# A decoder block on one core: the first group of down products by seven products, the residual's stores, the factors at the entry of the feed-forward part

## The chip, the core and the metric

The kernel runs on one core of a Trainium2 chip. The core has a matrix engine (TensorE, "PE" in the profile, with weight loads listed as "PEld"), a vector engine (VectorE, DVE), a scalar engine (ScalarE, ACT), a general one (GpSimd, POOL) and a queue engine (SyncE, SP); 16 DMA engines move data between HBM and the on-chip memory (SBUF). Matmul results go to eight PSUM banks. Each engine runs its own list of instructions in order and waits on semaphores for what the others deliver; the order in which the program is written sets only the order of each list.

The metric is the device time of one execution, in microseconds. Before the change the median of three runs is 2143.21 us (2142.64 to 2144.26).

## The reference, cut to what matters

The kernel computes one decoder block for 512 tokens of width 2048: a norm, one projection, two attention mixers, an output projection with residual, then a SwiGLU feed-forward part with residual and a last norm. All is float32. The part that matters here:

```python
hn2 = rmsnorm(h, norm2_g)                                        # 512 x 2048
h = h + (silu(hn2 @ w_gate) * (hn2 @ w_up)) @ w_down             # hidden width 5632
return rmsnorm(h, final_g)
```

## The kernel before, in words

A float32 product is made from three matmuls on rounded halves: each operand is split into a high part (ScalarE copies it rounded) and a low part (VectorE subtracts the high one), and high x high, high x low and low x high are added up in PSUM (`mm`, L1238 to L1241). Weights stream in as units of 512 KB (`load_to`, issued on SP, five buffers `raw`) and are split half a unit at a time by `Job` (128 x 512, lines L143 and L146); a split half is what the text calls a half. In the feed-forward part TensorE spends 12 matmuls of 256 columns on a half. `next_half` hands out split halves three ahead; `later(n, f)` places f behind the n-th next half in the program, `soon` and `tick` do so in steps of quarter products.

**Gate and up.** The hidden width is cut into 44 blocks of 128 (index f). For each, gate and up are made together as a 2 x 2 block product by seven products instead of eight (Strassen's scheme in Winograd's form): the left side is (gate, up) for the two halves of the input width, the right side the two halves of width by the two halves of the 512 tokens (256 each). `quad_jobs` lists the seven weight factors P1 to P7, which are sums of the four weight units A11, A21, A22 and A12. The sums are made in place by VectorE (`comb`, L819, and L843) or, in some blocks, by an adding load from HBM on POOL's queue (`fetch`, L823). The order of the seven is ORDER0 for f = 0, ORDER1 for f = 1 and for some later blocks, ORDER for the rest. With ORDER1 the factor A11 is restored by `fetch`, with ORDER all sums are VectorE's. `product` makes one of the seven (24 matmuls), `after` puts the results together on VectorE and ScalarE, `finish` applies silu and multiplies.

**Down.** The hidden blocks are grouped by four (PH = 4, eleven groups). The down product of groups 1 to 9 is made by seven products as well: `downs` places its 56 quarter products (8 output pairs k by seven names) into the schedule behind the last block of the group, `quarter` lists their weight factors, `down7` makes six matmuls each, copies partial sums between PSUM banks on ScalarE and sends the staged results to HBM tiles `kept_sums` by adding stores on POOL. `hidden_terms` builds the right-hand terms from the hidden values that `finish` left in `held`. At its first call `down7` makes two seeding matmuls (L1145). Group 0 is made plainly: in block 4 sixteen output blocks of 24 matmuls each (`down`), four behind each of the products from the fourth on, with weights from `wdn` in two buffers `rawd`, and its results are written to the same HBM tiles by plain stores. For it, `finish` splits the hidden values of blocks 0 to 3 straight into four 512-wide slots of `ah` and `al`. Group 10 is made plainly at the end (`last`).

**The residual.** It lies in SBUF (`hs`, 16 tiles of 128 x 512) until block 1. `put_away` stores a tile to HBM on POOL's queue: eight are placed behind P1 of block 1, one per half, eight behind P1 of block 2 (`AWAY`). The last one closes that memory and opens a pool of working tiles in its place (staging tiles `stga`, hidden values `hf`, terms `x3`), and clears one fifth of each `kept_sums` tile by a store of zeros. The residual is added into the sums in blocks 5, 6, 9, 10, 13, 14, 17 and 18 (`add_residual`), and all is brought back near the end.

**The entry.** In block 0, behind P6, two per-token factors are spread over partitions by matmuls (`Spread`): inv and r2, both copied from PSUM to SBUF by ScalarE (L282), with the loading of ScalarE's silu table in between (L1420). `after(0, "P6")` reads bank P1 times r2 on VectorE (L1302); block 1's first product writes that bank next.

Some first halves are split into buffers with another offset (`even`): block 2, each odd block, and the first quarter of a down group.

Of the kernel before, what the change touches and what calls it, by code (L numbers as in the profile page):

```python
# [16 lines left out]
S = 512  # L17
# [25 lines left out]
def plan():  # L43
# [31 lines left out]
def block_kernel(ctx: ExitStack, tc: tile.TileContext, xt, wst, wdn, smalls, wg, w2c, bias, ident_in, out):  # L75
# [711 lines left out]
    dn_loads = deque((0, nb) for nb in range(KB))  # L787
    dn = {}

    def load_dn():  # L790
        if dn_loads:
            k = dn_loads.popleft()
            dn[k] = wp.tile([128, 512], F32, tag="rawd", name="rawd", bufs=2)
            sp.dma_start(dn[k], wdn[k[0], k[1]])

# [15 lines left out]
    def quad_jobs(f, names):  # L811
# [17 lines left out]
        for k in range(2):  # L829
# [10 lines left out]
            elif order(f) == ORDER1:  # L840
# [29 lines left out]

    def dn_job(p, nb):
        return Job(lambda: dn[p, nb], post=load_dn)
# [38 lines left out]
    for f in range(FB):  # L911
        qj = quad_jobs(f, order(f))
        p = f // PH - 1
        nb = 0
        for i, name in enumerate(order(f)):
            seq = sorted(((k, n) for k in range(8) for n in DTIME), key=lambda x: 7 * x[0] + DTIME[x[1]])
            if name == "P3" and f > PH and f % PH == 0:
# [3 lines left out]
            if name == "P3" and f > PH and f % PH == 0:  # L921
# [14 lines left out]
    load_dn()  # L936
    load_dn()
# [9 lines left out]
    def close_attention():  # L947
# [16 lines left out]
        def close():  # L964
# [8 lines left out]
            for _ in range(2):  # L973
                ffn.tile([128, S], F32, tag="ft", name="ft", bufs=2)
# [42 lines left out]
    def ft(name="ft"):  # L1017
        return ffn.tile([128, S], F32, tag="ft", name=name, bufs=2)

# [89 lines left out]
    dbanks = {}  # L1109
    SEEDED = ("P6", "P7")  # L1110
    AWAY = {(1, "P1"): (0, 8, 0), (2, "P1"): (8, 8, 0)}
# [29 lines left out]
    def down7(p, k, name, wh, wl):  # L1141

        if not roles:
            seed = ps.tile([128, 512], F32, tag="misc", name="pd")
            pe.matmul(seed[:, :256], ones, sm[:, :1].to_broadcast([128, 256]), start=True, stop=True)  # L1145
            roles.append((banks["P3"], banks["P4"], seed, dbanks[1]))
# [13 lines left out]
        def add(x, q, n):  # L1160
            return lambda s=sums[x]: pool_e.dma_start(kept_sums[k][:, q:q + n, :], s, accum_op=OP.add)  # L1161
# [22 lines left out]
    def hidden_terms(f):  # L1184

        i = (f - 1) % 2
        x3 = st["x3"]
        hl = [[a[:, 12:16, :].rearrange("p t (i c) -> p t i c", c=256)[:, :, i, :] for a in (ah, al)],
              [a.rearrange("p (t i c) -> p t i c", i=2, c=256)[:, :, i, :] for a in x3]]
# [7 lines left out]
        if f % PH in (1, 2):  # L1197
            top = held[f - 1]
            t = st["pool"].tile([128, 1, 256], F32, tag="s2", name="t1", bufs=2)

            def s1():
                dve.tensor_tensor(t[:, 0, :], top[:, LO], top[:, HI], op=OP.subtract)
                hi(1, 2, 3, top[:, None, LO])

            def s2():
                lo(1, 2, 3, top[:, None, LO])
# [16 lines left out]
        def s2():  # L1223
            dve.scalar_tensor_tensor(t24[:, 0, :], t3[:, 0, :], -1.0, top[:, LO], op0=OP.mult, op1=OP.subtract)
            lo(0, 0, 2, botv)
            hi(0, 3, 4, t3)

        def s3():
            dve.scalar_tensor_tensor(t24[:, 1, :], t24[:, 0, :], -1.0, bot[:, LO], op0=OP.mult, op1=OP.subtract)
            lo(0, 3, 4, t3)  # L1230
# [12 lines left out]
    def finish(f, g, u, c):  # L1243
# [3 lines left out]
        wait = 0 if f == FB - 1 else 1 if f < 8 or f % PH else 2  # L1247
# [9 lines left out]
        def up():  # L1257
            if PH <= f <= FB - PH:
# [8 lines left out]
        if f < PH or f > FB - PH:  # L1267
# [10 lines left out]
    def after(f, name):  # L1278
# [11 lines left out]
        if name == "P1":  # L1290
            st["g"] = ft()
            if f:
                st["u"] = (st["pool"].tile([128, S], F32, tag="hf", name="hf", bufs=4)
                           if PH <= f <= FB - PH else ft())
# [28 lines left out]
    def down(ph, nb):  # L1323
        n = nb % 3
        if n not in dbanks:
            dbanks[n] = banks["P3"] if not n else (ps.tile([128, 512], F32, tag="t", name="pd", bufs=2) if n == 1 else
                                                ps.tile([128, 512], F32, tag="misc", name="pd"))
        p = dbanks[n]
        h, l = next_half()
        for c in (LO, HI):  # L1330
            for i in range(PH):
                mm(p[:, c], h[:, 128 * i:128 * i + 128], l[:, 128 * i:128 * i + 128], ah[:, 12 + i, c],
# [251 lines left out]
```

## Time and profile before

| | us |
|---|---|
| median of three runs | 2143.21 |
| the profiled execution | 2147.43 |
| its span, first to last instruction | 2145.6 |
| TensorE busy | 2128.1 |
| feed-forward blocks 0 to 8, start of block 0 to start of block 9 | 269.0 |

The profile is one execution. Times in it count from its first instruction. A row of the timeline gives start, length, engine, line, operation, output and inputs, shape, count, and in brackets the idle time of that engine ahead of it and what ended it. A row of windows gives a stretch, its length, and for each engine busy time and count of instructions (those that only reach into the stretch are counted too), then the granted TensorE clock, the DMA engines' busy share and GB/s. Matmuls overlap in the records (each is listed at 0.28 us, while they start 0.11 to 0.12 us apart), so the pace is read from counts and starts, not from durations. Buffer numbers are left out of names: the banks P1 to P7 are all "P".

### The profile page before, as it was taken

The page shows a single profiled execution, that of the slowest core. Times are in us where ns is not written, and L with a number is a line of the kernel's source. Part 1 is how long each engine was busy: PE and PEld are TensorE (multiplying, and loading weights), DVE is VectorE, ACT ScalarE, POOL GpSimd, SP SyncE. Part 2 cuts the span into 40 slices and gives each one's busy share as a digit, 9 for nine tenths or more (in the row PEclk, how much of TensorE's full clock was granted, in tenths as well). Part 3 has the DMA queues.
Part 4 walks back from the last instruction along what each step waited for, and adds up shares of the span by engine and source line. Part 5 has one row for each costly group of instructions (what it writes and reads, how often), then busy time and mean ns, then how long its engine had stood idle before and what let it go on. Part 6 is the DMA issues. An engine that isn't in the chain of part 4 may idle for free.

```text
span 2145.6 us, 41296 instructions
## 1 busy us (share of the span) xinstructions
PE 2128.1 (99%) x15346; PEld 1988.0 (93%) x15346; DVE 1629.4 (76%) x3460; ACT 1241.6 (58%) x2973; POOL 321.9 (15%) x378
## 2 busy tenths in 40 slices
PE   9999999999999999999999999999999999999997
PEld 7888888888888888999999999999999999999997
DVE  6755656366657678856989898898989898988885
ACT  6544444344445256444675858585767667675856
POOL 0000000000000001211131313131212213030323
PEclk9999999999999999999999999999999999999998
DMA  7442222322234334545596969775766758594982
GB/s 237 147 141 81 82 82 69 101 81 72 65 106 155 99 99 128 177 153 148 145 230 142 213 154 210 171 188 139 184 161 158 184 141 187 139 216 118 208 245 89
DMA packets 124347, 313.67 MB, mean 146 GB/s; under 512 B 13424, under 2 KB 35568, under 8 KB 124144
## 3 DMA queue, kind: packets, MB, share of 16 engines
q1 hardware_dynamic: 77104, 236.49, 34.9%
q0 software_dynamic: 46896, 74.47, 19.6%
q8 instruction: 120, 1.97, 0.4%
q14 instruction: 83, 0.68, 0.1%
q10 hardware_dynamic: 144, 0.07, 0.0%
HBM read 245.96 MB, written 65.01 MB: 145 GB/s over the span
## 4 chain that ended last, share of the span: by engine, by line
PE 96%; DMA 1%; DVE 1%; ACT 1%; issue 0%; SPq 0%; POOL 0%; DVEq 0%; ACTq 0%; POOLq 0%
PE P L1241 17%; PE P L1240 17%; PE P L1239 17%; PE pp L197 7%; PE pp L199 7%; PE pp L198 7%; PE pab L199 3%; PE pab L197 3%; PE pab L198 3%; PE pd L1239 2%; PE pd L1241 2%; PE pd L1240 2%; DMA raw<-in_wst_dram 1%; PE pt L568 1%; PE po L198 1%; PE pl L198 1%
## 5 line engine op out<-in xcount | busy, mean ns | idle before, releaser
L143 ACT ACTIVATE wh<-raw 128x512 fp32r<-128x512 f32 x888 | 532.7, 625 | 295.0 <-DVE raw L819 113.6
L146 DVE TENSOR_TENSOR wl<-raw,wh 128x512 fp32r<-128x512 f32 x888 | 599.3, 686 | 111.0 <-ACT wh L143 106.9
L1241 PE MATMUL P<-ah,wl 128*128 128x256 f32 x1536 | 426.1, 277 | 0.1
L1239 PE MATMUL P<-ah,wh 128*128 128x256 f32 x1536 | 425.2, 277 | 0.0
L1240 PE MATMUL P<-al,wh 128*128 128x256 f32 x1536 | 425.1, 277 | 0.0
L1241 PEld LDWEIGHTS P<-ah,wl 128*128 128x128 f32 x1536 | 288.3, 188 | 1.3 <-DVE wl L146 1.1
L1240 PEld LDWEIGHTS P<-al,wh 128*128 128x128 f32 x1536 | 288.4, 188 | 0.0
L1239 PEld LDWEIGHTS P<-ah,wh 128*128 128x128 f32 x1536 | 288.2, 188 | 0.0
L197 PE MATMUL pp<-ah,wh 128*128 128x512 f32 x640 | 260.5, 407 | 0.0
L199 PE MATMUL pp<-ah,wl 128*128 128x512 f32 x640 | 251.0, 392 | 0.0
L198 PE MATMUL pp<-al,wh 128*128 128x512 f32 x640 | 250.2, 391 | 0.0
L1161 POOL DMA_DIRECT2D sums<-stg x216 | 188.1, 927 | 312.0 <-ACT P L1155 150.0
L819 DVE TENSOR_TENSOR raw<-raw 128x512 f32<-128x512 f32 x270 | 185.7, 688 | 5.6 <-DMA raw<-in_wst_dram 2.0
L170 DVE TENSOR_TENSOR wl<-raw,wh 128x256 fp32r<-128x256 f32 x432 | 167.9, 420 | 27.3 <-ACT wh L166 25.8
L166 ACT ACTIVATE wh<-raw 128x256 fp32r<-128x256 f32 x432 | 159.2, 409 | 4.6 <-DVE raw L898 4.6
L199 PEld LDWEIGHTS pp<-ah,wl 128*128 128x128 f32 x640 | 120.2, 188 | 28.2 <-DVE wl L146 0.4
L197 PEld LDWEIGHTS pp<-ah,wh 128*128 128x128 f32 x640 | 120.5, 188 | 20.0 <-DVE tmp L369 0.5
L198 PEld LDWEIGHTS pp<-al,wh 128*128 128x128 f32 x640 | 120.6, 189 | 19.5
L555 ACT ACTIVATE e<-e,st 128x512 f32<-128x512 f32 (+1 forms) x96 | 53.7, 560 | 124.3 <-DVE st L549 124.3
L707 POOL TENSOR_TENSOR acc<-acc,osq 128x512 f32<-128x512 f32 x14 | 18.1, 1294 | 580.3 <-ACT osq L706 580.3
L1155 ACT ACTIVATE stg<-P 128x256 f32<-128x256 f32 x252 | 95.6, 381 | 12.7 <-PE P L1241 3.3
L197 PE MATMUL pab<-ah,wh 128*128 128x512 f32 x256 | 100.3, 392 | 0.0
(335 smaller groups left out, 5545.0 us busy)
## 6 DMA issues: line engine op xcount, KB each, us to landing
raw<-in_wst_dram SPq DMA_DIRECT2D x382, 512.0 KB, 4.2
sums<-stg POOLq DMA_DIRECT2D x160, 256.0 KB, 6.7
raw<-in_wst_dram POOLq DMA_DIRECT2D x42, 256.0 KB, 4.5
sums<-stg POOLq DMA_DIRECT2D x72, 128.0 KB, 6.3
bias<-in_bias_dram SPq DMA_DIRECT2D x16, 320.0 KB, 3.0
xc<-in_xt_dram SPq DMA_DIRECT2D x16, 256.0 KB, 3.5
rawd<-in_wdn_dram SPq DMA_DIRECT2D x16, 256.0 KB, 2.8
hs<-in_xt_dram SPq DMA_DIRECT2D x16, 256.0 KB, 5.7
```

Source lines behind the costliest of these rows:

```text
L143: act.activation(self.h, self.src(), AF.Copy)
L146: dve.tensor_tensor(self.l, self.src(), self.h.bitcast(F32), op=OP.subtract)
L166: act.activation(h, src(), AF.Copy)
L170: dve.tensor_tensor(l, src(), h.bitcast(F32), op=OP.subtract)
L197: pe.matmul(o, wh, mh, start=start, stop=False)
L198: pe.matmul(o, wh, ml, start=False, stop=False)
L199: pe.matmul(o, wl, mh, start=False, stop=stop)
L819: return lambda: dve.tensor_tensor(o(), o(), x(), op=OP.add)
L1161: return lambda s=sums[x]: pool_e.dma_start(kept_sums[k][:, q:q + n, :], s, accum_op=OP.add)
L1239: pe.matmul(o, wh, mh, start=start, stop=False, skip_group_check=True)
L1240: pe.matmul(o, wh, ml, start=False, stop=False, skip_group_check=True)
L1241: pe.matmul(o, wl, mh, start=False, stop=stop, skip_group_check=True)
```

## The change

- Group 0 is made like groups 1 to 9: `plan` puts its eight weight units behind block 4, the schedule calls `downs` for it, `down`, its loads and its buffers `rawd` go away, and `hidden_terms` runs from block 1 on. Its stores write instead of adding, so the clearing stores go away too. `finish` leaves blocks 0 to 3 in `held`; for their hidden values two working tiles `early` are added.
- The terms are assigned to other slots (P1 and P7 change places), so that those built in blocks 1 and 2 lie in `ah` and `al`; the difference that is built there stands in bank P3 instead of a working tile.
- The 16 stores of the residual are placed from P1 of block 1 on at 8i/5 halves, instead of eight and eight at one per half.
- Block 1 keeps ORDER1, but its factors are made as in the other form: P1 is followed by A11 + A21 on VectorE, P6 is preceded by A22 + A11 on VectorE, no `fetch`.
- In block 0 the silu table and r2 come ahead of inv, and inv's copy is placed five halves later.

```diff
-        if f > PH and f % PH == 0:
+        if f and f % PH == 0:
             p += [("dn", f // PH - 1, k) for k in range(8)]
...
-            elif order(f) == ORDER1:
+            elif order(f) == ORDER1 and f > 1:
...
-            if name == "P1" and f > PH + 1 and f % PH == 1:
+            if name == "P1" and f > PH and f % PH == 1:
                 downs(p, seq[-1:])
-            if f == PH and i > 2:
-                for _ in range(4):
-                    if nb < KB:
-                        sched.append(("d", p, nb))
-                        jobs.append(dn_job(p, nb))
-                        nb += 1
...
-    AWAY = {(1, "P1"): (0, 8, 0), (2, "P1"): (8, 8, 0)}
+    AWAY = {(1, "P1"): (0, 16, 0)}
...
-            return lambda s=sums[x]: pool_e.dma_start(kept_sums[k][:, q:q + n, :], s, accum_op=OP.add)
+            how = {"accum_op": OP.add} if p else {}
+            return lambda s=sums[x]: pool_e.dma_start(kept_sums[k][:, q:q + n, :], s, **how)
...
-            t = st["pool"].tile([128, 1, 256], F32, tag="s2", name="t1", bufs=2)
+            t = banks["P3"][:, None, :256]
...
-        wait = 0 if f == FB - 1 else 1 if f < 8 or f % PH else 2
+        wait = 0 if f == FB - 1 else 1 if f < PH or f % PH else 2
...
-            if PH <= f <= FB - PH:
+            if f <= FB - PH:
                 dve.scalar_tensor_tensor(u, u, -1.0, g, op0=OP.mult, op1=OP.mult)
                 held[f] = whole
...
-        if f < PH or f > FB - PH:
+        if f > FB - PH:
...
-            zero = pool.tile([128, 256], F32, tag="s2", name="zero", bufs=2)
-            pool_e.memset(zero, 0.0)
-            for k in range(8):
-                pool_e.dma_start(kept_sums[k][:, 2, :], zero)
...
-                later(at + i, lambda nb=first + i: put_away(nb))
+                later(at + 8 * i // 5, lambda nb=first + i: put_away(nb))
...
-        if PH < f <= FB - PH and name == order(f)[2]:
+        if 0 < f <= FB - PH and name == order(f)[2]:
...
-                st["inv"] = st["inv"]()
                 act.activation(st["rs2"].rs[:, 7, :1], ones[:, :1], AF.Silu)
                 st["r2"] = st["r2"](tag="t", bufs=2)
-                st["u"] = ft()
+                inv, pinv = st["inv"].r, st["inv"](False)
+                st["inv"] = inv
+                later(5, lambda: act.activation(inv, pinv, AF.Copy))
+                st["u"] = early()
```

More of the change, by code (lines that the diff above doesn't have):

```diff
@@ L972, in close @@
                                    for x, at in (("h", MH), ("l", ML)))
-            for _ in range(2):
-                ffn.tile([128, S], F32, tag="ft", name="ft", bufs=2)
+            for tag in ("ft", "early"):
+                for _ in range(2):
+                    ffn.tile([128, S], F32, tag=tag, name=tag, bufs=2)
             rest["hsp"] = ExitStack()
@@ L1018, in ft, with early @@
         return ffn.tile([128, S], F32, tag="ft", name=name, bufs=2)
+    def early():
+        return ffn.tile([128, S], F32, tag="early", name="early", bufs=2)
     sacc = ft("sacc")
@@ L1292, in after @@
             if f:
[L1293 to L1294 removed]
+                st["u"] = (ft() if f == 2 or f > FB - PH else early() if f == 1 else
+                           st["pool"].tile([128, S], F32, tag="hf", name="hf", bufs=4))
             else:
@@ L1321, in after @@
             finish(f, g, u, HI if f == FB - 1 else slice(0, 512))
[L1323 to L1332, printed above, removed]
-                   al[:, 12 + i, c], i == 0, i == PH - 1)
-        def add():
-            t = st["pool"].tile([128, 2, 256], F32, tag="stga", name="stg", bufs=3)
-            act.activation(t, p.rearrange("p (t c) -> p t c", c=256), AF.Copy, scale=1.0 if nb < 8 else -1.0)
-            pool_e.dma_start(mem_at(nb), t)
-        later(1, add)
     def mem_at(nb):
@@ L1379, in block_kernel @@
     for kind, a, b in sched:
-        if kind == "d":
-            down(a, b)
-            continue
         if kind == "s":
```

35 lines of the change are left out of this document (11 added, 24 removed).

## The prediction

> **What bounds the kernel now.** I read the first page, then the feed-forward part block by block (windows from one block's P1 to the next one's), then the idle time of TensorE, then the queues behind it. The page first:
>
> ```profile
> span 2145.6 us, 41296 instructions
> PE 2128.1 (99%) x15346; PEld 1988.0 (93%) x15346; DVE 1629.4 (76%) x3460; ACT 1241.6 (58%) x2973; POOL 321.9 (15%) x378
> PE 96%; DMA 1%; DVE 1%; ACT 1%; issue 0%; SPq 0%; POOL 0%; DVEq 0%; ACTq 0%; POOLq 0%
> ```
>
> TensorE is the bound: work taken from it is time, and so is each gap in it. The windows below are blocks 0, 1, 2, 3, 4 (with the first group's down products), 5, 6, 8 (second group) and 16 (fourth group). The columns are the stretch and its length, then busy time and count of each engine, granted clock, DMA share and GB/s.
>
> ```profile
> 836.00:859.61 23.61, 22.62 (x193) 22.42 (x191) 19.57 (x49) 17.90 (x39) 1.98 (x3) 1.00 0.49 134
> 859.61:878.84 19.23, 19.23 (x168) 19.23 (x169) 15.65 (x29) 8.81 (x17) 9.33 (x16) 1.00 0.60 183
> 878.84:903.68 24.84, 22.00 (x171) 21.49 (x170) 19.88 (x35) 11.90 (x24) 4.58 (x9) 0.93 0.69 241
> 903.68:923.49 19.81, 19.81 (x170) 19.81 (x169) 17.28 (x31) 10.59 (x21) 0.00 (x0) 1.00 0.37 108
> 923.49:988.50 65.01, 65.01 (x554) 65.01 (x553) 33.01 (x55) 28.68 (x53) 10.72 (x15) 1.00 0.44 146
> 988.50:1007.61 19.11, 19.11 (x170) 19.11 (x169) 13.27 (x24) 10.52 (x22) 1.95 (x2) 1.00 0.55 163
> 1007.61:1027.46 19.85, 19.84 (x171) 19.64 (x170) 17.81 (x34) 10.61 (x22) 2.39 (x2) 1.00 0.66 163
> 1046.57:1105.01 58.44, 58.44 (x502) 58.39 (x501) 51.23 (x118) 45.95 (x133) 20.18 (x24) 1.00 0.81 184
> 1280.33:1336.81 56.48, 56.48 (x500) 56.48 (x499) 50.74 (x117) 45.47 (x132) 20.03 (x24) 1.00 0.82 190
> ```
>
> A plain block holds 7 x 24 = 168 matmuls and needs 19.1 us (block 5); block 16 holds 168 + 55 x 6 = 498 in 56.48 us, 113.4 ns each. Block 2 is 5.7 us too long. Its gaps, in the order of time on TensorE (start, length, then the idle time in brackets and who ended it):
>
> ```profile
> 859.61 0.39 PE L1239 MATMUL P<-B11h,wh 128*128 128x256 f32 x1 [0.99 <-DVE ft L1302]
> ...
> 883.81 0.38 PE L1239 MATMUL P<-T4h,wh 128*128 128x256 f32 x1 [2.01 <-ACT wh L143]
> ...
> 885.14 0.39 PE L1241 MATMUL P<-T4h,wl 128*128 128x256 f32 x1 [0.83 <-DVE wl L146]
> ...
> 886.08 0.41 PE L1240 MATMUL P<-T4l,wh 128*128 128x256 f32 x1
> 886.29 0.41 PE L1241 MATMUL P<-T4h,wl 128*128 128x256 f32 x1
> ```
>
> Block 2's second product waits 2.01 and 0.83 us for its split weights, and then matmuls start 0.21 us apart (886.08 to 886.29) while the granted clock averages 0.93 over the block. The Trainium skill (TensorE: Matmul & The Clock Gate, Part 1) says that about 3.4 us of idling drops the array to half rate; here 2.8 us in two pieces were followed by it.
>
> Why are those weights late? DMA, in this order: the 10 us before the wait, the loads of block 1 (issued 844.0 to 854.4) with their times to landing, those of block 2 (871.0 to 876.3) with theirs, the residual's stores.
>
> ```profile
> 870.00:880.00 10.00, 10.00 (x90) 10.00 (x89) 6.80 (x12) 4.33 (x9) 5.42 (x11) 1.00 1.03 343
> ...
> L115 SPq DMA_DIRECT2D raw<-in_wst_dram x4: 328/328/328, 844.0 to 854.4; - x4
> DMA to landing us min/median/max: 3.6/3.7/3.7
> ...
> L115 SPq DMA_DIRECT2D raw<-in_wst_dram x4: 328/800/1400, 871.0 to 876.3; - x4
> DMA to landing us min/median/max: 7.7/9.7/10.9
> ...
> res<-hs POOLq DMA_DIRECT2D x14, 256.0 KB, 7.7
> ```
>
> The 16 engines are full, and four loads that take 3.7 us alone take 7.7 to 10.9 beside fourteen stores of 256 KB.
>
> A last fact: TensorE has two paces. Three stretches of 20 us, all at clock 1.00, in blocks 4, 8 and 16:
>
> ```profile
> 940.00:960.00 20.00, 20.00 (x172) 20.00 (x171) 6.20 (x10) 8.25 (x15) 4.30 (x6) 1.00 0.58 199
> 1070.00:1090.00 20.00, 20.00 (x172) 20.00 (x171) 17.49 (x45) 18.38 (x59) 10.47 (x13) 1.00 0.99 214
> 1290.00:1310.00 20.00, 20.00 (x179) 20.00 (x178) 19.74 (x47) 15.59 (x47) 3.52 (x4) 1.00 0.63 161
> ```
>
> 172 matmuls against 179: 4% slower, with no wait. Block 3 (19.81) and block 4 (65.01 / 552 = 117.8 ns) are in the slow pace, block 5 is out of it; so it follows block 2's gap and ends with the first half of block 5, an odd block.
>
> **The change, term by term.**
>
> *a. Group 0 by seven products.* Removed: 16 x 24 = 384 matmuls; added: 8 x 7 x 6 = 336, 330 of them in block 4 and 6 in block 5. Group 0 then is what groups 1 to 9 are. It will be the first to call the seven-product routine, so it takes over the two seeding matmuls, which now are in block 8:
>
> ```profile
> 1062.89 0.60 PE L1145 MATMUL pd<-sm,ones 128*128 128x256 f32 x2
> ```
>
> Block 8, with them and the slow pace behind them, is 58.44; block 16 is 56.48. I take 58.44 for block 4 and 19.11 + 6 x 0.1134 = 19.79 for block 5, against 65.01 + 19.11: **-5.9** (bounds: -7.9 with block 16's time, -5.0 with one more wait like block 6's, 19.85 - 19.11 = 0.7, and a little pace). What hides the extra splits, sums and terms: VectorE's 51 of 58 us and ScalarE's 46 as in block 8; here it has 33 and 29 now. Without that cover it would cost the difference, 18 us. The eight clearing stores fall away, the first group's stores overwrite instead of adding: off the path.
>
> *b. Block 2's gap.* In the program the 16 stores are placed over 26 halves from block 1's P1. But placing orders only each engine's own list. POOL's list of before:
>
> ```profile
> 837.78 0.86 POOL L823 DMA_DIRECT2D raw<-in_wst_dram  x1 [2.79 <-DVE wl L146]
> 838.32 1.44 POOL L1357 DMA_DIRECT2D res<-hs  x2
> 866.09 0.89 POOL L823 DMA_DIRECT2D raw<-in_wst_dram  x1 [26.32 <-issue]
> ```
>
> The two stores placed ahead of block 1's first adding load (L823) ran at 838.32, twenty microseconds before block 1 began; the rest sat behind that load until 866.09. The change takes both adding loads of block 1 out (its factors are now summed on VectorE), so nothing stands ahead of the stores: I expect them from 838.3 on, in a burst as before, 28 us earlier. 16 x 0.262 + 4 x 0.524 MB (block 1's loads) = 6.3 MB at 343 GB/s is 18 us: over by about 857. Block 2's loads then meet no store, and need not wait for the adding load either. Block 2 goes from 24.84 to block 5's 19.11: **-5.7** (bounds -5.7 and 0). If the stores did keep to their places, 262 KB each 26 x 1.36 / 16 = 2.2 us is 119 GB/s, with 2.1 MB of loads each 19 us (110 GB/s) 229 of 343: the gap would go too.
>
> *c. Block 3's pace.* No gap ahead of it: 19.81 to between 19.11 and 19.85 (block 6, the same order of products with a full VectorE, 17.81 of 19.85). VectorE gets the hidden terms there and keeps its eight weight sums, no less loaded than block 6: 19.3, **-0.5** (0 to -0.7).
>
> *d. Block 8* loses the seeding: 58.44 to 56.48 at best; half of it may come back through another wait: **-1.2** (0 to -2.0).
>
> *e. The start of block 1.* Its P1 waits for VectorE's L1302, which reads P1's bank times r2. The chain on ScalarE, then VectorE:
>
> ```profile
> 854.94 0.60 ACT L282 ACTIVATE r<-prb 128x512 f32<-128x512 f32 x1 [1.37 <-PE prb L279]
> 855.54 1.28 ACT L1420 ACT_TABLE_LOAD   x1
> 856.94 0.58 ACT L282 ACTIVATE r<-prb 128x512 f32<-128x512 f32 x1
> 857.42 2.18 ACT L143 ACTIVATE wh<-raw 128x512 fp32r<-128x512 f32 x4
> ...
> 854.67 0.68 DVE L146 TENSOR_TENSOR wl<-raw,wh 128x512 fp32r<-128x512 f32 x1
> 855.27 0.48 DVE L1036 SCALAR_TENSOR_TENSOR al<-hs,sm,ah 128x256 fp32r<-128x256 f32 x1
> 858.08 0.69 DVE L146 TENSOR_TENSOR wl<-raw,wh 128x512 fp32r<-128x512 f32 x1 [2.33 <-ACT wh L143]
> ```
>
> The first copy (inv) moves five halves back and the table load starts in ScalarE's 1.37 us of idling: r2 is ready some 1.9 us earlier. Against it two weight sums on VectorE ahead of L1302, some 0.6 us each pipelined (855.27 less 854.67 is such a step), one of them in VectorE's 2.33 us of idling. That alone clears the 0.99 us. But the first sum needs the second load of block 1, issued at about 847 and now inside the burst: landing by +3.7 it is early, by +9.7 it is there at 856.6, and the chain ends where it ends now. **-0.4** (-1.0 to +2).
>
> Block 1 itself stays at 19.2. Prices on VectorE, from blocks 5 to 7 (count, busy us, mean ns):
>
> ```profile
> L819 DVE TENSOR_TENSOR raw<-raw 128x512 f32<-128x512 f32 x15 | 10.3, 687 | 0.1
> L1195 DVE TENSOR_TENSOR al<-t,ah 128x256 fp32r<-128x256 f32 x3 | 1.3, 419 | 0.0
> ```
>
> It gains two sums (1.4 us) and three pieces of terms in place of one 512-wide piece (3 x 0.42 - 0.69 = 0.6) on 15.65 of 19.23: room for it. The difference that now lies in a bank instead of SBUF has the same 256 columns. The working tiles that open behind the last store lie on the residual's memory; ScalarE and VectorE write them first in block 3, with weight splits queued behind: no wait if the stores end at 857, nor if the last goes out 35 us after 859.6 and takes 7.7 (903, block 3's first halves). Sum: -5.9 - 5.7 - 0.5 - 1.2 - 0.4 = **-13.7 us**. The profiled execution took 2147.43 (span 2145.6), so 2133.7 there; it is 4.2 above the median 2143.21, which by the same sum gives 2129.5. Block 2's gap may be a little smaller unprofiled: I say **2130**.
>
> **The rivals.**
>
> *R1, the gap only moves.* The burst meets block 1's loads as it now meets block 2's. For it: they are issued 844 to 854, inside 838 to 857. Against: the first is needed only at the end of block 0, and the last two are issued when the burst is nearly over. Price: block 2's loss of 5.7 less the 1.0 lost there already, in place of e: -13.7 + 0.4 + 4.7 = -8.6, 2134.6. The Trainium skill (DMA: Bandwidth & Descriptors, "Issuing engines are not separate DMA queues") speaks for it: POOL's and SP's transfers run on the same 16 engines and interleave; the 7.7 to 10.9 us above agree.
>
> *R2, block 2 keeps its gap* (POOL held up by something that this trace doesn't show): without b and c, -7.5, 2135.7. Against: POOL's own rows above.
>
> *R3, slower: the slow pace stays.* Buffers move in SBUF (two loading buffers out, two working tiles in), operands change places, and the pace that an odd block's first half restored at 988.50 was not restored at 903.68 (19.81). If it stayed on from block 1 to the end, 1100 us at 7/179 = 3.9% would cost 43 us, less the 0.7 + 2.4 + 2.0 that blocks 3, 4 and 8 pay already: 38 - 13.7, about 2167. It decides from 13.7 / 0.039 = 350 us of slow pace more than now. Against: blocks 5 and 16 left it in this same layout of weights.
>
> *R4, nothing much*: b absent and the seven products' own waits, each like block 6's 0.7 in several blocks, eat a: 2139 to 2147.
>
> **How the numbers follow.** Forecast 0.66, R1 0.14, R2 0.08, R3 0.06, R4 0.06. The forecast's own bounds: all terms at their best, -7.9 - 5.7 - 0.7 - 2.0 - 1.0 = -17.3 or 2126; at their worst but b whole, -5.0 - 5.7 - 0 - 0 + 2 = -8.7 or 2134.5. R1 and R2 add to that up to 2140; a microsecond is left under 2126. Range 2125 to 2140. 0.2% is 4.3 us, about what can be told from no change: faster (under 2138.9) 0.88, the same 0.05 (most of R4), slower 0.07 (R3 and a rest).
>
> **What would show it.** Right: block 4's window at 56.5 to 58.5 and block 5's at 19.8; block 2's near 19.1 with clock 1.00 and no wait on ScalarE's L143; POOL's stores in one run from about 838; 179 matmuls in 20 us between 900 and 940; block 8 under 58. Wrong: stores strung over 860 to 895 (b's mechanism, not its size), a wait over 2 us at block 1's P1 with half clock behind it (R1), 172 in 20 us beyond block 9 (R3), waits on VectorE's L146 in blocks 3 and 4 (c and a).

## The result, and the profile after

| | before | after |
|---|---|---|
| median, us | 2143.21 | 2132.82 |
| lowest and highest of seven runs each, us | 2141.71 to 2149.80 | 2129.82 to 2137.18 |
| the profiled execution, us | 2147.43 | 2129.82 |
| its span, us | 2145.6 | 2127.9 |
| start of block 0 to start of block 9, us | 269.0 | 254.5 |

The ratio is 0.995 (95% interval 0.9934 to 0.9967): faster by 10.4 us at the median, inside the range, 2.8 us above the forecast of 2130. The two profiled executions differ by more, 17.6 us, because the one of before lay 4.2 us above its median and the one of after lies 3.0 us below (17.6 - 4.2 - 3.0 = 10.4). Why executions of one program scatter by several microseconds is taken up at the end. Two of the runs below, x_inv and x_even, contain one execution of 5501 us each, which is left out of their ratios and moves their medians by under 0.2 us.

The page of after, first its span, the busy time of each engine, and the shares of the chain of waits:

```profile
span 2127.9 us, 41370 instructions
PE 2115.0 (99%) x15298; PEld 1976.8 (93%) x15298; DVE 1653.4 (78%) x3540; ACT 1260.1 (59%) x3059; POOL 317.0 (15%) x375
PE 99%; DVE 1%; issue 0%; ACT 0%; DVEq 0%; ACTq 0%
```

There are 15346 - 15298 = 48 matmuls fewer, the 384 less 336 of group 0. The chain is TensorE's at 99%, where it was 96%: DMA, POOL and the queues of SP and POOL have left it. VectorE got 24 us more to do and ScalarE 18.5; their shares of the chain have not grown.

The windows of after, blocks 0 to 5 and 8, columns as before:

```profile
835.47:858.11 22.64, 22.63 (x193) 22.42 (x191) 20.84 (x51) 17.00 (x38) 9.50 (x17) 1.00 0.91 302
858.11:877.33 19.22, 19.22 (x168) 19.22 (x169) 18.68 (x36) 11.38 (x23) 0.00 (x0) 1.00 0.32 96
877.33:896.45 19.12, 19.12 (x170) 19.12 (x169) 17.06 (x31) 10.52 (x22) 0.00 (x0) 1.00 0.40 126
896.45:915.57 19.12, 19.12 (x170) 19.12 (x169) 18.25 (x34) 11.40 (x23) 0.00 (x0) 1.00 0.33 103
915.57:974.75 59.18, 59.13 (x502) 58.88 (x501) 52.04 (x119) 46.05 (x132) 11.68 (x22) 1.00 0.59 177
974.75:994.54 19.79, 19.79 (x176) 19.79 (x175) 16.61 (x30) 11.60 (x25) 2.53 (x4) 1.00 0.65 200
...
1033.50:1089.98 56.48, 56.48 (x501) 56.48 (x499) 50.82 (x117) 45.16 (x131) 20.09 (x24) 1.00 0.81 190
```

Block 2 is a plain block of 19.12 us at clock 1.00: its gap is gone, and so is the slow pace of block 3. Block 4 took 59.18 us in place of 65.01, block 8 dropped to 56.48.

POOL's timeline of after, all that it started from 837.79 us to block 4, then the stores in the DMA list of after (size of one transfer in KB, then median us from issue to landing), then block 2's loads with their times to landing:

```profile
837.79 4.62 POOL L1321 DMA_DIRECT2D res<-hs  x8
843.43 4.17 POOL L1321 DMA_DIRECT2D res<-hs  x7 [1.01 <-DMA res<-hs]
848.20 0.54 POOL L1321 DMA_DIRECT2D res<-hs  x1 [0.60 <-DMA res<-hs]
```

```profile
res<-hs POOLq DMA_DIRECT2D x16, 256.0 KB, 6.6
```

```profile
L115 SPq DMA_DIRECT2D raw<-in_wst_dram x4: 328/328/794, 869.0 to 873.9; - x4
DMA to landing us min/median/max: 3.5/4.2/4.9
```

The stores were placed from block 1's P1 on, 1.6 halves apart. They ran from 837.79, twenty microseconds before block 1 began, in 11 us, with two short waits for an earlier one to land. The last two lines are block 2's four loads. They were issued when the stores had long landed and took 3.5 to 4.9 us, where they had taken 7.7 to 10.9 us before.

### The profile page after: what moved, and what is told of

It reads as the page before. It is cut to its first block, busy times and chain, and to the rows that moved or that the text cites. A ratio compares the mean times of both kernels' runs of the same rounds, so it can differ in the third digit from the quotient of the medians.

```text
span 2127.9 us, 41370 instructions
## 1 busy us (share of the span) xinstructions
PE 2115.0 (99%) x15298; PEld 1976.8 (93%) x15298; DVE 1653.4 (78%) x3540; ACT 1260.1 (59%) x3059; POOL 317.0 (15%) x375
## 3 DMA queue, kind: packets, MB, share of 16 engines
HBM read 245.43 MB, written 65.01 MB: 146 GB/s over the span
## 4 chain that ended last, share of the span: by engine, by line
PE 99%; DVE 1%; issue 0%; ACT 0%; DVEq 0%; ACTq 0%
PE P L1224 18%; PE P L1222 18%; PE P L1223 18%; PE pp L197 7%; PE pp L199 7%; PE pp L198 7%; PE pab L197 3%; PE pab L198 3%; PE pab L199 3%; PE pd L1222 1%; PE pd L1224 1%; PE pd L1223 1%; PE pt L568 1%; PE pl L198 1%; PE po L198 1%; PE po L197 1%
## 5 line engine op out<-in xcount | busy, mean ns | idle before, releaser
L146 DVE TENSOR_TENSOR wl<-raw,wh 128x512 fp32r<-128x512 f32 x888 | 598.6, 685 | 99.9 <-ACT wh L143 96.8
L1224 PE MATMUL P<-ah,wl 128*128 128x256 f32 x1616 | 447.6, 277 | 0.1
L1222 PE MATMUL P<-ah,wh 128*128 128x256 f32 x1616 | 447.3, 277 | 0.0
L1223 PE MATMUL P<-al,wh 128*128 128x256 f32 x1616 | 446.9, 277 | 0.0
L1224 PEld LDWEIGHTS P<-ah,wl 128*128 128x128 f32 x1616 | 303.4, 188 | 1.1 <-DVE wl L146 1.1
L1222 PEld LDWEIGHTS P<-ah,wh 128*128 128x128 f32 x1616 | 303.4, 188 | 0.0
L1223 PEld LDWEIGHTS P<-al,wh 128*128 128x128 f32 x1616 | 303.3, 188 | 0.0
L1144 POOL DMA_DIRECT2D sums<-stg x240 | 201.0, 889 | 426.7 <-ACT P L1137 149.3
L170 DVE TENSOR_TENSOR wl<-raw,wh 128x256 fp32r<-128x256 f32 x480 | 186.4, 419 | 29.3 <-ACT wh L166 27.7
L810 DVE TENSOR_TENSOR raw<-raw 128x512 f32<-128x512 f32 x274 | 188.1, 686 | 3.6
L166 ACT ACTIVATE wh<-raw 128x256 fp32r<-128x256 f32 x480 | 176.6, 409 | 4.8 <-DVE raw L886 4.8
L1137 ACT ACTIVATE stg<-P 128x256 f32<-128x256 f32 x280 | 106.2, 382 | 13.7 <-PE P L1224 2.7
```

The costliest lines, as they stand in the source:

```text
L146: dve.tensor_tensor(self.l, self.src(), self.h.bitcast(F32), op=OP.subtract)
L166: act.activation(h, src(), AF.Copy)
L170: dve.tensor_tensor(l, src(), h.bitcast(F32), op=OP.subtract)
L810: return lambda: dve.tensor_tensor(o(), o(), x(), op=OP.add)
L1222: pe.matmul(o, wh, mh, start=start, stop=False, skip_group_check=True)
L1223: pe.matmul(o, wh, ml, start=False, stop=False, skip_group_check=True)
```

## The experiments

Each run comes with runs of the kernel before on the same chip: 2144.56 us by the median for x_entry, x_seven, x_fetch and x_place, 2146.08 for x_spread, x_order, x_even and x_res, 2145.06 for x_inv, x_again, x_reseven and x_best. The kernel after was timed apart from these, so between sets the ratios are compared, not the times. Where a wait of TensorE is given below, it is that of the weight load (PEld) unless matmuls are named; the matmul behind it shows 0.2 us less.

**The two halves of the change, each alone.** *x_entry* is the kernel before with the stores' placing, block 1's factors and the order of the entry:

```diff
-            elif order(f) == ORDER1:
+            elif order(f) == ORDER1 and f > 1:
...
-    AWAY = {(1, "P1"): (0, 8, 0), (2, "P1"): (8, 8, 0)}
+    AWAY = {(1, "P1"): (0, 16, 0)}
...
-                later(at + i, lambda nb=first + i: put_away(nb))
+                later(at + 8 * i // 5, lambda nb=first + i: put_away(nb))
...
-                st["inv"] = st["inv"]()
                 act.activation(st["rs2"].rs[:, 7, :1], ones[:, :1], AF.Silu)
                 st["r2"] = st["r2"](tag="t", bufs=2)
+                inv, pinv = st["inv"].r, st["inv"](False)
+                st["inv"] = inv
+                later(5, lambda: act.activation(inv, pinv, AF.Copy))
```

> The kernel before with the new placing of the stores, block 1's factors summed on VectorE and the new order of r2 and inv, group 0 still plain. Theory (POOL freed by taking out the adding loads): stores in one run from 838 us, block 2 19.1 us, block 3 19.1, block 4 at the fast pace 168 + 384 matmuls x 0.1134 = 62.6 us, block 1 starts 1 us earlier; 9 to 10 us less than before in the profile, that is 2134 by the median. Rival (most of the gain comes from the seven products): block 2 still over 22 us, 1 to 3 us less than before.

*x_seven* is the kernel after with these four places put back, so that only group 0 by seven products, with the slots that its terms need, remains.

> The changed kernel with the adding loads of block 1, the old placing of the stores and the old order of r2 and inv; only group 0 by seven products is left of the change. Theory: block 2 keeps its gap (24 to 25 us, clock below 1.00), block 4 about 58 to 59 us, block 8 56.5 us; 5 to 8 us less than before (2135 to 2138). Rival (the gap in block 2 came from the plain form's own splits and loads): block 2 at 19.1 us and 2130.

Windows of x_entry, blocks 2, 4 and 8:

```profile
877.08:896.20 19.12, 19.12 (x171) 19.12 (x169) 17.04 (x30) 10.62 (x22) 0.00 (x0) 1.00 0.39 123
915.32:977.88 62.56, 62.56 (x555) 62.56 (x553) 32.84 (x55) 28.61 (x53) 10.73 (x15) 1.00 0.47 152
1035.43:1093.87 58.44, 58.44 (x502) 58.39 (x501) 51.04 (x117) 45.75 (x132) 20.17 (x24) 1.00 0.82 186
```

and of x_seven, blocks 0, 2, 4 and 8:

```profile
835.47:859.09 23.62, 22.63 (x194) 22.42 (x192) 19.59 (x49) 17.89 (x39) 1.99 (x3) 1.00 0.49 134
878.30:902.45 24.15, 22.00 (x171) 21.38 (x169) 19.84 (x37) 12.00 (x25) 0.69 (x2) 0.93 0.57 207
922.26:981.35 59.09, 59.09 (x502) 59.03 (x501) 51.79 (x118) 45.97 (x132) 11.87 (x22) 1.00 0.57 176
1040.10:1096.58 56.48, 56.48 (x501) 56.48 (x499) 50.80 (x117) 45.53 (x132) 20.05 (x24) 1.00 0.82 191
```

x_entry took 2137.36 us (ratio 0.9967, 0.9954 to 0.998): 7.2 less than before, with block 2's gap gone and block 8 as it was. x_seven took 2137.14 (0.9968, 0.9956 to 0.998): 7.4 less, with the gap in place and block 8 at 56.48. Both halves are real and of like size. x_entry's 2134 was not reached at the median, though its block 2 and block 4 came as expected. The halves are not additive: in blocks 0 to 8 of the profiles they give 10.3 and 7.9 us, 18.2 together, where the whole change gave 14.5. The largest part of that is x_entry's plain block 4, 552 matmuls in 62.56, which is in the fast pace, 2.45 less than the 65.01 that it took behind block 2's gap.

**What let the stores go.** *x_fetch* is the kernel after, its wide placing kept, with block 1's two adding loads back:

```diff
-            elif order(f) == ORDER1 and f > 1:
+            elif order(f) == ORDER1:
```

> The changed kernel with the two adding loads of block 1 back, everything else as changed, the placing over 26 halves too. Theory: POOL's list again has two to four stores, an adding load, stores, an adding load and then the rest; the rest runs from about 865 us in one burst whatever the placing says, block 2 is 22 to 25 us, 4 to 6 us slower than the changed kernel. Rival (the wider placing spreads the stores in time): stores 2.2 us apart from 865 to 895, block 2 19.1 us, time as the changed kernel's.

*x_place* keeps the loads out and has the old placing, eight and eight at one per half:

```diff
-    AWAY = {(1, "P1"): (0, 16, 0)}
+    AWAY = {(1, "P1"): (0, 8, 0), (2, "P1"): (8, 8, 0)}
...
-                later(at + 8 * i // 5, lambda nb=first + i: put_away(nb))
+                later(at + i, lambda nb=first + i: put_away(nb))
```

> The changed kernel with the old placing of the stores (eight from block 1, eight from block 2, one per half), the rest as changed. Theory: the placing sets no time, POOL runs ahead: stores in one run from 838 us, every block within 0.1 us of the changed kernel, time the same. Rival (the placing matters): stores start with block 1 at 859 us, block 2 longer than 20 us, 2 to 6 us slower than the changed kernel.

POOL's timeline of x_fetch, its window of block 2, and the times to landing of block 2's four loads:

```profile
838.00 1.45 POOL L1321 DMA_DIRECT2D res<-hs  x2
863.82 0.89 POOL L814 DMA_DIRECT2D raw<-in_wst_dram  x1 [24.37 <-issue]
...
865.66 4.10 POOL L1321 DMA_DIRECT2D res<-hs  x7
```

```profile
877.96:900.85 22.89, 21.04 (x170) 20.07 (x169) 18.26 (x35) 12.01 (x25) 0.00 (x0) 1.00 0.57 199
...
DMA to landing us min/median/max: 7.6/9.1/11.0
```

and those of x_place:

```profile
837.65 5.15 POOL L1321 DMA_DIRECT2D res<-hs  x9
843.96 3.50 POOL L1321 DMA_DIRECT2D res<-hs  x6 [1.16 <-DMA res<-hs]
...
```

```profile
877.21:896.33 19.12, 19.12 (x171) 19.12 (x169) 17.09 (x31) 10.52 (x22) 0.00 (x0) 1.00 0.38 114
```

This separates the two edits that the change puts together. With the adding loads back, two stores run at 838, the other fourteen sit behind the loads until 865.66, block 2's loads take 7.6 to 11.0 us, and block 2 is 22.89 - 19.12 = 3.8 us too long, in spite of the wide placing (24.15 with the old placing and the old entry, in x_seven). Without the adding loads the stores burst and block 2 is whole, in either placing. x_fetch took 2136.37 (0.9961, 0.9949 to 0.9973), 3.3 above x_place on the same chip, a little less than the 4 to 6 that were expected. x_place took 2133.05 (0.9951, 0.9937 to 0.9964), the ratio of after. Its blocks 0 to 3 are within 0.02 us of after's; blocks 4, 7, 8 and 12 are not within the expected 0.1 (57.65, 19.81, 58.66 and 58.66 against 59.18, 19.11, 56.48 and 56.48), which is taken here for the scatter treated at the end, since x_again, which is after itself, differs by as much in block 4. Once the loads are gone, the spreading of the stores over 26 halves does nothing: POOL's list has nothing in it that would hold a store to its place.

**Does the burst cost anything?** *x_spread* issues the stores from ScalarE, on whose list weight splits stand between them, so that they are held to their places (they also go through another queue then):

```diff
-        pool_e.dma_start(kept_hs[nb], hs[:, nb, :])
+        act.dma_start(kept_hs[nb], hs[:, nb, :])
```

> The changed kernel with the residual's 16 stores issued from ScalarE's list instead of POOL's, so that they really go out over the 26 halves. Theory (a store out of the way of the loads is all that matters, and 229 GB/s do not fill the engines): stores about 2.2 us apart from 860 to 895 us, block 2 at 19.1 us with clock 1.00, block 1's wait at its P1 0.1 us or less instead of 0.18; the time within 0.1% of the changed kernel. Rival (loads and stores side by side delay block 2 in any case): block 2 over 20 us, 1 to 4 us slower.

ScalarE's queue in x_spread, first and last store, with a weight split between them, and the windows of blocks 0 and 2:

```profile
863.01 0.33 ACTq L1321 DMA_DIRECT2D res<-hs  x1
...
877.01 0.63 ACT L143 ACTIVATE wh<-raw 128x512 fp32r<-128x512 f32 x1 [2.06 <-DMA raw<-in_wst_dram]
...
894.94 0.33 ACTq L1321 DMA_DIRECT2D res<-hs  x1
```

```profile
835.61:858.26 22.65, 22.63 (x193) 22.42 (x191) 20.86 (x51) 17.00 (x38) 0.86 (x1) 1.00 0.48 116
877.48:897.56 20.08, 19.91 (x171) 19.72 (x169) 17.69 (x33) 11.54 (x25) 0.00 (x0) 1.00 0.79 272
```

Now the stores are strung over 863 to 895. Block 0 takes 22.65 with no burst in it and 22.64 with the burst: the burst costs block 0 nothing. Block 2 pays 1.0 us. Its loads take 4.4 to 6.9 us beside the stores, the split shown waits 2.06 us for one, VectorE is 1.1 us later in the block than in after, and TensorE's third product waits 0.36 us and goes on in the slow pace. So block 2 came out as the rival had it, over 20 us, and not at 19.1; the 1 to 4 us of the rival do not show in the total. x_spread took 2129.96 (0.993, 0.9916 to 0.9943); the interval overlaps after's, which decides nothing.

**The entry.** *x_inv* is the kernel after with inv copied first again, ahead of the table and r2, as before the change (the last part of x_entry's diff, reversed).

> The changed kernel with the old order in block 0 (inv spread and copied first, then the table, then r2). Theory (r2's lateness alone makes block 1's first product wait): block 0 at 23.6 us instead of 22.65, the wait at its end 1.0 to 1.2 us; 1.0 us slower. Rival (the stores' burst or the new weight sums set that start): block 0 at 22.7 us, no difference; or the burst adds to it and block 0 is at 24.5.

Its window of block 0, the first weight load of block 1's P1, and the same load in after:

```profile
835.67:860.01 24.34, 22.63 (x193) 22.42 (x191) 20.94 (x51) 17.90 (x39) 9.50 (x17) 1.00 0.85 281
```

```profile
860.01 0.19 PEld L1222 LDWEIGHTS P<-B11h,wh 128*128 128x128 f32 x1 [1.92 <-DVE ft L1285]
```

```profile
858.11 0.19 PEld L1222 LDWEIGHTS P<-B11h,wh 128*128 128x128 f32 x1 [0.22 <-DVE ft L1285]
```

VectorE's rows of x_inv ahead of that load:

```profile
857.75 0.69 DVE L146 TENSOR_TENSOR wl<-raw,wh 128x512 fp32r<-128x512 f32 x1 [1.60 <-ACT wh L143]
858.48 0.69 DVE L810 TENSOR_TENSOR raw<-raw 128x512 f32<-128x512 f32 x1
```

With x_fetch's block 0 this makes a square (us of block 0): old order without the sums 23.62 (x_seven), old order with them 24.34 (x_inv), new order without them 22.47 (x_fetch), new order with them 22.64 (after). The new order is worth 1.15 without the sums and 1.70 with them; the two weight sums cost 0.72 in the old order and 0.17 in the new one. The run's expectation had left the sums out of the old order. The rows show that its rival, the burst, is not what came on top: the second sum (L810 at 858.48) follows directly on the split that VectorE waited for, with no wait for a load, and it is one sum's length that block 0 grew by. x_inv took 2135.78 (0.9951, 0.9937 to 0.9964), 4.2 above x_again on the same chip where 1.0 was expected. The 1.70 us of block 0 are in that, but this profile also has slow blocks late in the program (24 to 26, 33 and 34) that x_again's has not.

Block 1 shows that a wait does not always do harm. In after, x_inv and x_fetch alike the last matmuls of block 0 start 118 ns apart. In the first two TensorE then waits 0.22 and 1.92 us, and block 1 takes 19.22 us in both; in x_fetch it does not wait, the slow pace goes on, and block 1 takes 19.81.

**Block 4's extra time.** In after one wait stands in block 4, 5.6 us from its start. The timeline of after around it (VectorE, ScalarE, TensorE's weight load):

```profile
920.11 0.68 DVE L810 TENSOR_TENSOR raw<-raw 128x512 f32<-128x512 f32 x1
920.71 0.68 DVE L146 TENSOR_TENSOR wl<-raw,wh 128x512 fp32r<-128x512 f32 x1
...
920.88 0.63 ACT L143 ACTIVATE wh<-raw 128x512 fp32r<-128x512 f32 x1 [0.69 <-DVE raw L810]
...
921.45 0.19 PEld L1224 LDWEIGHTS P<-ah,wl 128*128 128x128 f32 x1 [0.24 <-DVE wl L146]
```

VectorE has run without a pause since 911.9 and is late. Its weight sum (L810) keeps ScalarE's split waiting for 0.69 us, and the low half that it makes next (L146, done at 921.4) is what TensorE waits for, 0.24 us. *x_order* gives blocks 3 and 4 the order of products ORDER1, which takes two weight sums in each off VectorE (adding loads make them) and puts the others elsewhere; *x_even* leaves the wait but splits one more early half of group 0 into a shifted buffer:

```diff
-        return ORDER0 if not f else ORDER1 if f == 1 or 4 < f <= FB - PH and f % PH in (3, 0) else ORDER
+        return ORDER0 if not f else ORDER1 if f == 1 or 2 < f <= FB - PH and f % PH in (3, 0) else ORDER
```

```diff
-                    downs(p, seq[n:n + 2])
+                    downs(p, seq[n:n + 2], not p and n == 1)
```

> The changed kernel with ORDER1 and its adding loads for blocks 3 and 4 too (two weight sums fewer on VectorE in each). Theory (VectorE, 18.3 of 19.1 us in block 3, is late for block 4's third product): the wait of 0.3 us at 5.6 us into block 4 goes, the fast pace holds to the seeding, block 4 at 58.4 us; 0.8 us less. Rival (VectorE is not what that wait hangs on, or the adding loads cost as much): a wait in block 3 or 4 stays, block 4 58.8 us or more.

> The changed kernel with the shifted buffers also for the second pair of quarter products of group 0, the first that is split behind the seeding matmuls. Theory (the seeding and the wait at block 4's third product leave TensorE in the slow pace, and a half from shifted buffers brings the fast one back): block 4 at 57.3 us or less instead of 59.2, 179 matmuls in 20 us between 945 and 965; about 1.7 us less. Rival (the slow pace belongs to the down group's operands or to DMA load, not to what went before): 172 in 20 us, block 4 59 us, no change.

Block 4 in x_order, then in x_even:

```profile
915.48:973.92 58.44, 58.44 (x502) 58.39 (x501) 51.08 (x117) 45.88 (x132) 13.66 (x24) 1.00 0.65 192
```

```profile
915.15:972.55 57.40, 57.34 (x503) 57.09 (x501) 51.92 (x119) 45.67 (x132) 11.56 (x22) 1.00 0.61 182
```

In x_order TensorE is busy for all of the 58.44: no wait, and only the slow pace behind the seeding, the very time that block 8 had before. In x_even the wait is there and the fast pace comes back behind it twice. The first time, right behind the wait, is not the edit's doing: the shifted half comes only behind the seeding, and x_fetch, without the edit, has the same. The second time is. x_fetch and x_even enter the seeding at the same pace; here are 20 us of block 4 from 23 us on, x_fetch, then x_even:

```profile
943.00:963.00 20.00, 20.00 (x172) 20.00 (x172) 17.29 (x45) 18.46 (x60) 6.29 (x12) 1.00 0.73 230
```

```profile
938.00:958.00 20.00, 20.00 (x179) 20.00 (x178) 18.02 (x47) 19.01 (x61) 6.48 (x13) 1.00 0.77 231
```

x_order against x_best, below, is the same pair without the wait: 172 and 179. In all three kernels with the edit (x_even, x_reseven, x_best) the pace came back at that half. Of the nine other profiles with this block, three came back as well (x_again, x_place, x_spread, at 57.7 us), so 59.2 is not what block 4 costs in every execution. In the time of the whole neither edit shows: 2132.0 (0.9933, 0.9919 to 0.9946) and 2133.54 (0.9947, 0.9932 to 0.9963).

**The pair of blocks 5 and 6.** Block 6 took 19.85 in before and after alike, with a wait of 0.2 us on VectorE's low half, some 4 us behind a residual tile that VectorE scales. *x_res* scales the odd tiles five halves later, so that they leave the first products of blocks 6, 10, 14 and 18:

```diff
-        later(4, scale)
+        later(9 if nb % 2 else 4, scale)
```

> The changed kernel with the odd residual tiles scaled nine halves behind P7 instead of four, that is at the fifth half of the next block instead of its first. Theory (in blocks 6, 10, 14 and 18 that scaling makes VectorE late for the third product, and the wait leaves the slow pace behind, which in some executions outlasts block 7 and then the down group): these blocks at 19.1 us instead of 19.8, blocks 7, 8, 11 and 12 always at 19.1 and 56.5; 3 us less than the changed kernel's fastest runs and 4 to 5 less by the median, with less scatter. Rival (the scatter and the slow pace are not set off by these waits): 19.8 us as before or the same median.

Block 6 in after, then in x_res:

```profile
994.54:1014.39 19.85, 19.84 (x171) 19.64 (x169) 17.80 (x34) 10.60 (x22) 2.40 (x2) 1.00 0.67 164
```

```profile
994.65:1013.69 19.04, 19.04 (x171) 19.04 (x169) 17.79 (x34) 10.53 (x22) 2.40 (x2) 1.00 0.66 159
```

The same instructions, without the wait, 0.8 us less, in each of the four blocks (19.04 in all of them); blocks 7, 8, 11 and 12 are at 19.1 and 56.5 in this profile. The run took 2128.17 (0.9915, 0.9903 to 0.9928). Its four times lie within 1.9 us of each other, where the seven of after lie within 7.4 and the five of x_again within 3.5. It has no run of the kernel after on its own chip, so the 4 to 5 us that were expected against that kernel are not settled by it; x_reseven, below, has one.

**The kernel after once more, and the versions put together.** *x_again* is the kernel after unchanged, beside *x_reseven* (x_res and x_even) and *x_best* (x_res, x_even and x_order).

> The changed kernel once more, beside the others on one chip. Theory (the scatter of 2129.8 to 2137.2 is the slow pace, which lasts for another set of blocks in each execution): in this profile each block is either at its fast time (19.1, 19.8, 56.5 us) or 0.7 us (single blocks) or 1.3 to 2.2 us (down groups) above it, and the sum of these explains the span against 2127.9 to within 1 us; median 2132 to 2134. Rival: the difference lies elsewhere, in the attention part before 836 us or in waits on DMA.

> The changed kernel with the later scaling of the odd residual tiles and the shifted buffers for the second pair of group 0. Theory: block 4 at 57.4 us, blocks 6, 10, 14 and 18 at 19.1; 2126.5 by the median, 1.7 us under the version with the later scaling alone (2128.2). Rival (the two share one effect): 2128.

> The same with ORDER1 for blocks 3 and 4 as well. Theory: no wait in blocks 1 to 19 but the 0.2 us at block 1's start and the seeding's 0.3; block 4 at 56.9 us; 2126 by the median, the fastest of all. Rival (the adding loads of blocks 3 and 4 bring a wait of their own): 2127 or more.

| | median, us | lowest to highest | ratio to before |
|---|---|---|---|
| x_again | 2131.62 | 2128.73 to 2132.22 | 0.9934 (0.9922 to 0.9947) |
| x_reseven | 2128.05 | 2126.88 to 2128.66 | 0.9919 (0.9905 to 0.9933) |
| x_best | 2124.58 | 2123.47 to 2125.87 | 0.9905 (0.9892 to 0.9919) |

x_again's span is 2128.2, after's 2127.9, so there was hardly a difference left to explain. It is made of larger ones that cancel: block 4 1.5 less, blocks 6 and 18 0.5 less each, block 32 1.5 more, blocks 41 and 42 0.7 more each, and 0.55 less ahead of block 0, where the rival looked. Single blocks stand between the times that were expected: 57.65 in block 4, 19.31 in block 6.

x_reseven missed the time that was expected of it and took its rival's, 2128: block 4 is at 57.39, but that is only 0.26 under x_again's on the same chip, and blocks 12 and 28 were slow (58.20 and 58.82). All its runs are still below all of x_again's. x_best beats both kernels: 20.5 us under before and 7.0 under after on the same chip, all its runs below all of theirs. Its windows of blocks 4 and 9:

```profile
915.88:972.96 57.08, 57.08 (x503) 57.03 (x501) 50.77 (x117) 45.65 (x132) 13.57 (x24) 1.00 0.67 195
...
1087.40:1107.97 20.57, 20.57 (x176) 20.40 (x175) 17.28 (x32) 12.02 (x26) 3.99 (x5) 1.00 0.90 218
```

Block 4 has no wait and the pace comes back early. Block 9, with its 20.57, has one more short wait (0.17 us) that was not expected, and block 10 behind it is slow too (19.78).

## Why the prediction was right, point by point

By the profiled executions, blocks 0 to 8 gave 14.5 us where the sum said 13.7:

| term | forecast | measured | how |
|---|---|---|---|
| a, blocks 4 and 5 | -5.9 | -5.15 | 59.18 + 19.79 against 65.01 + 19.11 |
| b, block 2 | -5.7 | -5.7 | 19.12 against 24.84 |
| c, block 3 | -0.5 | -0.7 | 19.12 against 19.81 |
| d, block 8 | -1.2 | -2.0 | 56.48 against 58.44 |
| e, end of block 0 | -0.4 | -1.0 | 22.64 against 23.61 |

- **The sum** is closer than its terms: a fell short by 0.75, while b to e together gave 1.5 more than forecast.
- **b** came by the mechanism on record: x_fetch and x_place show that the adding loads on POOL's list, not the stores' places, made the gap. The side remark that stores held to their places would remove the gap too was nearly right: x_spread leaves 1.0 us of it.
- **a** was mis-sized by 0.75 us in this profile. The step at fault is the 58.44 for block 4, which charged the seeding's pace and no wait of the block's own; there is one, from VectorE, which the prediction expected to have room, with the slow pace behind it. Of the signs on record, 59.18 is over the 58.5 named for block 4, the 179 matmuls in 20 us held from 900 to 920 and not from 920 to 940 (168), and the wait on L146 in block 4 had been named as a sign of being wrong. x_order takes the wait away and gives 58.44. The bound with one more wait (-5.0) held. x_again, with the same wait, took 57.65 in block 4, which would make a -6.7, so the size of this term changes from one execution to the next.
- **d**: the half that "may come back through another wait" did not; block 8 has none.
- **e**: the step that failed is the burst. The second load of block 1 was feared at the end of the burst; issued at 846.3 it took 8.0 us, as long as loads beside the stores took before (7.7 to 10.9), and yet its sum ran at 854.86 on VectorE, in time for the read of P1's bank (L1285 in after) at 857.63. x_spread shows the same block 0 without the burst. What the two sums cost (0.17 us) and what the order saves (1.70) is x_inv's square.
- **The rivals.** R1 is out: 0.22 us at block 1's P1, clock 1.00. R2 needed POOL to be held up by something unseen; it was not. R4's wait does exist in block 4 (block 6's was there before), but it ate 0.75, not all of a. R3, the slow pace that stays, did not come at its size, yet it is the one that lives on in the scatter.
- **The rest.** Of the profiled difference of 17.6 us, 3.1 lie outside blocks 0 to 8: 0.5 ahead of block 0, the rest behind block 8. The prediction put nothing there, and its 2133.7 for the profiled execution is 3.9 too high mostly for that. The largest piece is block 12, 58.35 before and 56.48 after. Nothing in the change touches block 12. It is slow in four of the fourteen profiles (before, x_entry, x_place, x_reseven), so this is taken for scatter, and the medians, which hold many such blocks, are the measure: -10.4 here and -13.4 (2145.06 to 2131.62) in x_again. The forecast of -13.7 is at the edge of the first interval and within the second. That it is as near as this to the median is in part luck, since the scatter of one program is as large as its error. Whether the true effect is nearer 10 or 13 the runs do not settle.

## What to carry to other kernels

A place in the program binds an instruction only if its engine has something to wait for there: read on the engine's own list what stands ahead of it, because taking that away moves everything behind it. When TensorE is busy 99% of the time, look for waits of a fifth of a microsecond, since the pace that follows can cost several times the wait (0.8 us for 0.2 in block 6), and compare by several runs, since one profile can lie several microseconds off its median. Test the two sides of a change apart: here each was worth 7 us, and one edit that looked central (the spreading) was worth nothing once the adding loads were gone.

## What the runs showed of the hardware

**A wait of 0.2 us can leave TensorE 4% slower, and whether it recovers differs between executions of one program.** The same 20 us of block 4, first of after, then of x_again, the same program:

```profile
943.00:963.00 20.00, 20.00 (x172) 20.00 (x172) 16.34 (x41) 18.12 (x59) 6.48 (x12) 1.00 0.81 252
```

```profile
943.00:963.00 20.00, 20.00 (x179) 20.00 (x178) 17.38 (x45) 18.83 (x61) 7.11 (x14) 1.00 0.81 255
```

Both had a wait of 0.24 us at about 921 and were slow behind it, at clock 1.00 and with no further wait. In x_again the starts come closer together behind the seeding matmuls (932), which leaves 179 in the window; after stayed at 172. Block 4 took 57.65 in the one and 59.18 in the other. Block 6 is alike: both wait 0.2 us, x_again is back at 113 ns at once (19.31 us), after stays at 118 (19.85). The first half of an odd block, with its shifted buffer, does not restore the pace each time either. Block 7 of x_place, and block 8 behind it, against 19.11 and 56.48 in after:

```profile
1012.74:1032.55 19.81, 19.81 (x170) 19.81 (x169) 17.84 (x34) 11.59 (x23) 2.94 (x3) 1.00 0.68 153
1032.55:1091.21 58.66, 58.66 (x501) 58.66 (x500) 50.71 (x117) 45.74 (x132) 20.20 (x24) 1.00 0.80 182
```

That is 2.9 us from a pace carried over out of block 6, with no wait in either block; x_place's profiled execution (2137.75 us) is the slowest of its five. What decides between recovery and not stays open, apart from the shifted half behind the seeding, which brought the pace back three times out of three. That x_res, which takes away four of the waits, has the smaller scatter fits, but rests on four runs.

**Half clock behind short waits in one run, not in another.** In x_seven TensorE's matmuls waited twice in block 2:

```profile
882.58 0.38 PE L1222 MATMUL P<-T4h,wh 128*128 128x256 f32 x1 [1.31 <-ACT wh L143]
...
883.91 0.38 PE L1224 MATMUL P<-T4h,wl 128*128 128x256 f32 x1 [0.83 <-DVE wl L146]
```

The window that follows 1.3 us later had a granted clock of 0.52 for 3.4 us:

```profile
885.20:888.60 3.40, 3.40 (x17) 3.17 (x16) 3.21 (x7) 1.72 (x4) 0.00 (x0) 0.52 0.11 42
```

In x_fetch waits of 0.83, 0.25 and 0.70 us, 1.8 in sum and spread over 881.5 to 886.9, left the clock at 1.00 in the whole of block 2. The Trainium skill (TensorE: Matmul & The Clock Gate, Part 1) describes activity judged over windows of about 3.4 us that run freely; the length of the half-clock stretch agrees, and x_seven adds that idling need not fill such a window: 2.1 us of it within 2.6 us were followed by the half clock. Whether x_fetch was spared by the smaller sum or by the spreading these runs do not separate.
